# Value pass of a two-layer decoder trunk: a pair of chunks every five chunks, with the sums of rows made by accumulating transfers

## The chip, the core and the metric

The kernel runs on one core of one Trainium2 chip. A core has five engines with a queue of instructions each, which wait for each other only through semaphores: PE (TensorE, matrix products), DVE (VectorE), ACT (ScalarE), POOL (GpSimd) and SP (SyncE, which here only issues transfers). Sixteen DMA engines move data between HBM and the on-chip memory. The metric is device time of one execution in microseconds, lower is better.

## The reference, cut to what matters

Two layers; each is a token mixer with cross-attention, and then a channel mixer (`peer_ffn`) that picks 16 of 16384 experts per token and head and adds up their value rows:

```python
u = u_tab[eid]
act = gelu(einsum('nhkd,nd->nhk', u, xb))
coef = gw * act
return einsum('nhk,nhkd->nd', coef, v_tab[eid])
...
x = layer_norm(DN_ALPHA * x + y, ln2_g[i], ln2_b[i])
```

There are 256 tokens of 1024 channels, and everything is float32. The kernel does not gather rows. It computes a dense table of coefficients, 16384 experts by 256 tokens, zero where an expert was not chosen, and multiplies it with the whole table `v`. That product, 256 tokens x 16384 experts x 1024 channels, is the value pass.

## The kernel before, in words

`peer_layer` streams the table `u` in 128 chunks, then the table `v` in 128 chunks of 128 experts x 1024 channels (512 KB each). All float32 products are made in three passes: each operand is split into a rounded high part (ACT casts it, line 110 for a chunk, line 246 for coefficients) and the remainder (DVE subtracts, line 125 and line 247), and `mm3` (lines 184 to 186) adds high x high, high x low and low x high.

The value pass is the loop over `i` in `range(P)` from line 1285. In step `i`:

- `next` pumps the stream. It splits chunk `i + 2` into a buffer pair `wH`, `wL` (three of them, `HL_BUFS`), and issues on SP's queue as many loads as the five `raw` buffers allow (`RAW_BUFS`, counted by `n_flight`).
- `coef(i + 2)` splits the coefficients of chunk `i + 2`: 256 columns, 128 for each half of the tokens. They lie in `lo` (chunks 0 to 63) and `hi` (64 to 127), which are also free scratch space once a chunk has been used.
- `paired(i)` does the additional work for pairs, below.
- PE multiplies chunk `i`: two halves of tokens (`tt`) x two halves of channels x three passes = 12 matmuls with 512 columns, all accumulated in four banks of PSUM.

The order on each engine is the order in which this code issues; nothing is reordered. ACT and DVE can be two chunks ahead of PE, since a split waits only for the buffer that PE has finished with.

Pairs. Two neighbouring chunks `p` and `p + 1` form a two-by-two block product (two halves of tokens, two chunks, two halves of channels), which normally takes eight block products. For a pair the kernel takes seven, by the scheme of Strassen and Winograd: it needs four sums of coefficients `s` (128 columns each) and four sums of rows `t` (512 columns each), all split into high and low parts: `sh`, `sl`, `th`, `tl`, which live in `xHL`. Four of the products use sums; their results go to banks of their own (`m1`, `m5`, `m7`, `m6`), which DVE and ACT add into the result once after the last pair (`onto`, counted from `done`). With a0, a1 for the two halves of channels of chunk `p`, and b0, b1 for those of chunk `p + 1`, the row sums are t1 = a1 - a0, t3 = b1 - a1, t2 = t3 + a0 and t4 = b0 - t2. `owed` says in which step PE makes the four products of sums.

Before, a pair sits at chunks 8k + 2 and 8k + 3: 12 values of k in layer 0 (`PAIRS[0]`, without 10) and 13 in layer 1. DVE makes the four row sums in two steps from the two raw chunks (lines 1197, 1198, 1200 and 1201), which keep their `raw` buffers until then.

In layer 0 the stream also carries four parts of the memory tokens (`memT`, split by ACT and POOL, line 123) and four pieces of `wkv` (split by ACT and DVE), after the chunks listed in `MEM1`: 80, 82, 84, 86 and 113, 116, 119, 122. At step `CLOSE - 2` the pool that holds `lo` is closed, and its space goes to the buffers for these.

Of the kernel before, what the change touches and what calls it, by code (L numbers as in the profile page):

```python
# [8 lines left out]
F32R = mybir.dt.float32r  # L9
# [4 lines left out]
ALU = mybir.AluOpType  # L14
# [36 lines left out]
class Trunk:  # L51
# [32 lines left out]
    def pump(self, upto):  # L84
        nc = self.nc
        upto = min(upto, len(self.items))
        while self.n_split < upto:
            i = self.n_split
            self.load(i + 1)
            ap, n, dest, keep, cuts = self.items[i]  # L90
            r = self.loaded.pop(i)
            self.n_split += 1
            if keep is not None:
                self.kept[keep] = r
                continue
            if type(dest) is int:
                h, l = self.extra[dest]
            elif dest is None:
                h = self.hl.tile([P, D], F32R, name="wH")[:, :n]
                l = self.hl.tile([P, D], F32R, name="wL")[:, :n]  # L100
            else:
                h, l = dest()
            z = self.twin.get(i)
            if z is not None:
                if z == 0:
                    self.pair = [r, self.loaded[min(q for q in self.twin if q > i)]]
                n = min(n, 512 * (z + 1))
                cuts = [slice(0, n)]
            for c in cuts:
                (nc.vector.tensor_copy if self.cast_dve else nc.scalar.copy)(h[:, c], r[:, c])  # L110
            k = n if getattr(dest, "pool", False) else min(n, self.pool_cols)
            if len(cuts) > 1:
                for c in cuts:
                    e = (nc.vector, nc.gpsimd)[c.start > 0]
                    e.tensor_sub(l[:, c], r[:, c], h[:, c].bitcast(F32))
                k = n
            elif k and self.chained:
                nc.vector.tensor_sub(l[:, k:], r[:, k:], h[:, k:].bitcast(F32))  # L118
                k += 2
                nc.gpsimd.tensor_sub(l[:, :k], r[:, :k], h[:, :k].bitcast(F32))  # L120
                k = n
            elif k:
                nc.gpsimd.tensor_sub(l[:, :k], r[:, :k], h[:, :k].bitcast(F32))  # L123
            if k < n:
                rest = lambda l=l, r=r, h=h, c=slice(k, n): nc.vector.tensor_sub(l[:, c], r[:, c], h[:, c].bitcast(F32))  # L125
# [912 lines left out]
    def peer_layer(self, layer):  # L1038
        nc, tc, A = self.nc, self.tc, self.A
        with ExitStack() as ctx:  # L1040
# [118 lines left out]
            first = {8 * k + 2: k for k in PAIRS[layer]}  # L1159
            done = 8 * PAIRS[layer][-1] + 8  # L1160
            gl = cp.tile([P, T], F32, name="gl", bufs=1)
            th, tl = self.xHL[:, 0:3, :], self.xHL[:, 3:6, :]
            sh, sl = (self.xHL[:, f, :].rearrange("p (f t) -> p f t", f=4) for f in (6, 7))
            plain = lambda a: a.bitcast(F32)

            def sums32(k):
                old = hi if k > 8 else lo
                flat = lambda b: old[:, b:b + 2, :].rearrange("p a b -> p (a b)")
                return [flat(b) for b in (0, 2, 4, 6)], flat(8).rearrange("p (f t) -> p f t", f=4)

            def split_sums(k, f, n, s):
                old = hi if k > 8 else lo
                t = old[:, 2 * f:2 * (f + n), :].rearrange("p (f a) b -> p f (a b)", f=n)
                nc.vector.tensor_sub(tl[:, s:s + n], t, plain(th[:, s:s + n]))

            def cast_sums(k, f, n, s):
                old = hi if k > 8 else lo
                t = old[:, 2 * f:2 * (f + n), :].rearrange("p (f a) b -> p f (a b)", f=n)
                nc.scalar.copy(th[:, s:s + n], t)

            def paired(i):
                k, j = divmod(i, 8)
                if j == 0 and k - 1 in PAIRS[layer]:
                    cast_sums(k - 1, 3, 1, 0)
                if j == 7 and k + 1 in PAIRS[layer]:
# [5 lines left out]
                    nc.vector.tensor_add(s[:, 0], ua, ub)  # L1191
                if k in PAIRS[layer]:
                    t, s = sums32(k)
                    if j < 2:
                        (a0, a1), (b0, b1) = [[r[:, :512], r[:, 512:]] for r in self.pair]
                    if j == 0:
                        nc.vector.tensor_sub(t[0], a1, a0)
                        nc.vector.tensor_sub(t[1], b1, a1)
                    elif j == 1:
                        nc.vector.tensor_add(t[2], t[1], a0)  # L1200
                        nc.vector.tensor_sub(t[3], b0, t[2])
                        self.n_flight -= 2
                        self.load(len(self.items))
                    elif j == 4:
                        nc.scalar.copy(sh[:, 0:3], s[:, 0:3])
                        nc.scalar.copy(sh[:, 3], part(i - 1)[1])
                        nc.vector.tensor_sub(sl[:, 0:3], s[:, 0:3], plain(sh[:, 0:3]))
                        nc.vector.tensor_sub(sl[:, 3], part(i - 1)[1], plain(sh[:, 3]))
                        cast_sums(k, 0, 2, 0)
                    elif j == 5:  # L1210
                        split_sums(k, 0, 2, 0)
                        cast_sums(k, 2, 1, 2)
                    elif j == 6:
                        split_sums(k, 2, 1, 2)
                if j == 0 and k - 1 in PAIRS[layer]:
                    split_sums(k - 1, 3, 1, 0)
                q = hi[:, 0:2, :].rearrange("p a b -> p (a b)")

                def onto(t, h, src, scale=ALPHA):
# [21 lines left out]


            owed = {}
            for k, n in zip(PAIRS[layer], PAIRS[layer][1:] + [None]):
                e = 8 * k + 7
# [6 lines left out]
            def coef(i):  # L1252
                src = block(i)
                if i in first:
                    cH, cL = cp.tile([P, T], F32R, name="cH"), cp.tile([P, T], F32R, name="cL")
                    self.split_to(cH[:, :P], cL[:, :P], src[:, :P])
                    return cH, cL
                if i - 1 in first:
                    cH, cL = cp.tile([P, T], F32R, name="cH"), cp.tile([P, T], F32R, name="cL")
                    _, s = sums32(i // 8)  # L1260
                    nc.scalar.copy(cH[:, :P], src[:, :P])
                    nc.scalar.copy(cH[:, P:], s[:, 3])
                    nc.vector.tensor_sub(cL[:, :P], src[:, :P], plain(cH[:, :P]))
                    nc.vector.tensor_sub(cL[:, P:], s[:, 3], plain(cH[:, P:]))
# [20 lines left out]
            for i in range(P):  # L1285
# [22 lines left out]
                if i in first or i - 1 in first:  # L1308
                    (_, (h, l), (cH, cL)), = late
                    if i in first:  # L1310
                        mixed(m1, h[:, :512], l[:, :512], (cH[:, :P], cL[:, :P]), first[i])
# [7 lines left out]
                for k, m in owed.get(i, ()):  # L1319
                    if m == 3:  # L1320
                        mixed(y[1][0], th[:, 0], tl[:, 0], (sh[:, 3], sl[:, 3]))
                    else:
                        mixed((m5, m7, m6)[m], th[:, m], tl[:, m], (sh[:, m], sl[:, m]), k)
                late = []
            self.pool_cols = MIX_COLS
            if layer:
# [22 lines left out]
    def plan(self):  # L1349
# [24 lines left out]
        def tail(layer):  # L1374
# [7 lines left out]
                self.add(A["u"][layer, i], D)  # L1382
            for i in range(P):
                e = i - P + HL_BUFS + EXTRA
                if i % 8 in (2, 3) and i // 8 in PAIRS[layer]:
                    self.twin[len(self.items)] = i % 8 - 2
# [113 lines left out]
```

## Time and profile before

| | |
|---|---|
| median of 3 runs | 1813.54 us (1813.49 to 1814.55) |
| the profiled execution | 1813.66 us, span 1811.9 us |
| granted TensorE clock | 0.999 |
| PE busy | 1791.1 us, 99% of the span |
| DVE, ACT, POOL busy | 80%, 55%, 24% |
| read from HBM | 330.98 MB |
| SP-issued queue | 56.9% of 16 DMA engines over the span |

The span runs from the first to the last instruction; the execution's own time has some launch and end around it. Busy shares are averages over stages with different limits: in the search stages DVE and POOL have more to do, in the value pass less. The value pass of layer 0 runs from about 577 to 922 us, that of layer 1 from about 1461 to 1804 us. A row of a group of instructions gives line, engine, operation, output and inputs, shapes, count, then busy time in us, mean ns of one, and the idle time of its engine just before it with what ended that.

### The profile page before, as it was taken

The numbers are of one execution on the slowest core, as the hardware profiler recorded it, in microseconds if no ns is written. First come the engines' busy times: TensorE is split into PE (matmuls) and PEld (weight loads), VectorE is DVE, ScalarE is ACT, GpSimd is POOL, SyncE is SP. The second block draws the span as 40 slices with busy tenths as digits, with TensorE's granted clock in tenths as the row PEclk, the third lists the DMA queues.
The fourth block names the chain that finished last, engine by engine and source line by source line (L and its number), as shares of the span: only waits on it lengthen the run. The fifth ranks groups of instructions, "written<-read, shape, count | busy, mean of one in ns | idle before, by whom it ended". The sixth has DMA issues, their size and how long they took to land.

```text
span 1811.9 us, 33750 instructions
## 1 busy us (share of the span) xinstructions
PE 1791.1 (99%) x12735; PEld 1652.1 (91%) x12735; DVE 1451.5 (80%) x3035; ACT 993.4 (55%) x1766; POOL 430.9 (24%) x324
## 2 busy tenths in 40 slices
PE   8999999999999999999999999999999999999998
PEld 8999999999999888888898899999999988888886
DVE  6674769599998888878868748685999978888877
ACT  6554555455545666566657355555554456665653
POOL 2015772333332000010001368325333300000000
PEclk9999999999999999999999999999999999999999
DMA  7656565655555655565756355666555556555564
GB/s 241 208 160 193 172 194 191 197 167 163 162 164 164 208 198 198 197 210 190 243 177 186 114 179 177 197 191 186 161 163 164 164 175 212 198 199 192 186 209 128
DMA packets 95555, 334.22 MB, mean 184 GB/s; under 512 B 10652, under 2 KB 13728, under 8 KB 95136
## 3 DMA queue, kind: packets, MB, share of 16 engines
q1 hardware_dynamic: 93752, 328.93, 56.9%
q10 hardware_dynamic: 1640, 3.15, 0.5%
q8 instruction: 99, 1.62, 0.4%
q14 instruction: 64, 0.52, 0.1%
HBM read 330.98 MB, written 1.05 MB: 183 GB/s over the span
## 4 chain that ended last, share of the span: by engine, by line
PE 71%; issue 17%; POOL 7%; DVE 3%; ACT 1%; DMA 0%; POOLq 0%; SPq 0%; DVEq 0%; ACTq 0%
PE bank L186 23%; PE bank L185 23%; PE bank L184 23%; POOL wL L120 7%; PE bank L250 2%; ACT wH L110 1%; DVE eL L125 0%; DVE wL L125 0%; PE bank L344 0%; DVE eH L110 0%; POOL wL L123 0%; PE bank L243 0%; DMA raw<-in_w0kg_dram 0%; DMA cp<-in_rg_par_dram 0%; DVE x L297 0%
## 5 line engine op out<-in xcount | busy, mean ns | idle before, releaser
L110 ACT CAST wH<-raw 128x1024 fp32r<-128x1024 f32 (+3 forms) x605 | 615.9, 1019 | 689.6 <-PE bank L186 222.1
L184 PE MATMUL bank<-xHL,wH 128*128 128x256 f32 x2536 | 715.6, 282 | 5.0 <-ACT wH L110 5.0
L186 PE MATMUL bank<-xHL,wL 128*128 128x256 f32 x2536 | 702.2, 277 | 0.6 <-DVE wL L125 0.6
L185 PE MATMUL bank<-xHL,wH 128*128 128x256 f32 x2536 | 702.4, 277 | 0.0
L125 DVE TENSOR_TENSOR wL<-raw,wH 128x1024 fp32r<-128x1024 f32 (+3 forms) x413 | 451.7, 1096 | 276.1 <-ACT wH L110 274.4
L184 PEld LDWEIGHTS bank<-xHL,wH 128*128 128x128 f32 x2536 | 477.3, 188 | 5.0 <-ACT wH L110 5.0
L186 PEld LDWEIGHTS bank<-xHL,wL 128*128 128x128 f32 x2536 | 477.1, 188 | 1.1 <-DVE wL L125 0.8
L185 PEld LDWEIGHTS bank<-xHL,wH 128*128 128x128 f32 x2536 | 477.9, 188 | 0.0
L185 PE MATMUL bank<-wL,cH 128*128 128x512 f32 x890 | 346.4, 389 | 1.0 <-DVE wL L125 1.0
L186 PE MATMUL bank<-wH,cL 128*128 128x512 f32 x890 | 346.7, 390 | 0.0
L184 PE MATMUL bank<-wH,cH 128*128 128x512 f32 x890 | 345.9, 389 | 0.0
L123 POOL TENSOR_TENSOR wL<-raw,wH 128x1024 fp32r<-128x1024 f32 (+1 forms) x121 | 256.0, 2120 | 209.3 <-ACT wH L110 208.8
L185 PEld LDWEIGHTS bank<-wL,cH 128*128 128x128 f32 x890 | 167.0, 188 | 37.7 <-DVE wL L125 2.5
L186 PEld LDWEIGHTS bank<-wH,cL 128*128 128x128 f32 x890 | 167.0, 188 | 35.3
L184 PEld LDWEIGHTS bank<-wH,cH 128*128 128x128 f32 x890 | 167.1, 188 | 35.0
L120 POOL TENSOR_TENSOR wL<-raw,wH 128x386 fp32r<-128x386 f32 x126 | 129.8, 1030 | 279.8 <-DVE wL L118 279.8
L333 POOL TENSOR_TENSOR x<-x,raw 128x256 f32<-128x256 f32 x6 | 4.9, 819 | 545.9 <-ACT x L330 545.9
L1000 DVE TENSOR_TENSOR oh<-iota,i12T 128x1024 f16<-128x1024 f16 x128 | 130.5, 1019 | 0.0
L118 DVE TENSOR_TENSOR wL<-raw,wH 128x640 fp32r<-128x640 f32 x126 | 104.0, 825 | 7.4
L1003 DVE TENSOR_TENSOR oh<-oh,gT 128x1024 f16<-128x1024 f16 x128 | 90.0, 703 | 4.4
L1133 PE MATMUL bank<-oh 128*128 128x128 f16 x1024 | 81.1, 220 | 1.1 <-DVE oh L1003 1.1
L1133 PEld LDWEIGHTS <-oh 128*128 128x128 f16 x1024 | 58.9, 98 | 6.0 <-DVE oh L1003 1.5
(340 smaller groups left out, 1989.8 us busy)
## 6 DMA issues: line engine op xcount, KB each, us to landing
raw<-in_u_dram SPq DMA_DIRECT2D x256, 512.0 KB, 3.6
raw<-in_v_dram SPq DMA_DIRECT2D x256, 512.0 KB, 4.1
raw<-in_w_q_dram SPq DMA_DIRECT2D x32, 512.0 KB, 4.2
raw<-in_w_out_dram SPq DMA_DIRECT2D x16, 512.0 KB, 4.0
raw<-in_w0qx_dram SPq DMA_DIRECT2D x8, 512.0 KB, 5.0
raw<-in_wkv_dram SPq DMA_DIRECT2D x8, 512.0 KB, 5.7
raw<-in_w0v_dram SPq DMA_DIRECT2D x8, 384.0 KB, 5.7
raw<-in_w0o_dram SPq DMA_DIRECT2D x8, 384.0 KB, 3.0
```

Source lines behind the costliest of these rows:

```text
L110: (nc.vector.tensor_copy if self.cast_dve else nc.scalar.copy)(h[:, c], r[:, c])
L118: nc.vector.tensor_sub(l[:, k:], r[:, k:], h[:, k:].bitcast(F32))
L120: nc.gpsimd.tensor_sub(l[:, :k], r[:, :k], h[:, :k].bitcast(F32))
L123: nc.gpsimd.tensor_sub(l[:, :k], r[:, :k], h[:, :k].bitcast(F32))
L125: rest = lambda l=l, r=r, h=h, c=slice(k, n): nc.vector.tensor_sub(l[:, c], r[:, c], h[:, c].bitcast(F32))
L184: mm(out, sH, mH, start=start, stop=False, skip_group_check=True)
L185: mm(out, sH, mL, start=False, stop=False, skip_group_check=True)
L186: mm(out, sL, mH, start=False, stop=stop, skip_group_check=True)
L250: self.nc.tensor.matmul(out, lhsT, rhs, start=start, stop=stop, skip_group_check=True)
L1000: nc.vector.tensor_tensor(flat(oh[:, 1:3]), self.iota2.unsqueeze(1).to_broadcast([P, 4, P, 2]), pairs(self.i12T[:, j]), op=ALU.is_equal)
L1003: nc.vector.tensor_tensor(flat(oh[:, 0:2]), two.rearrange("p z (q e t) -> p z q e t", q=2, t=2), pairs(self.gT[:, j]), op=ALU.mult)
L1133: nc.tensor.matmul(wp[:, qs], oh[:, 2, q // 2, :, q % 2], oh[:, z, q // 2, :, q % 2], start=z == 0, stop=z == 1, skip_group_check=True)
```

## The change

Pairs now start at chunk 8 and then at every fifth chunk from 16: up to 96 in layer 0 (18 pairs) and up to 106 in layer 1 (20 pairs).

The row sums are no longer made by DVE. At step p - 2 SP loads a0 a second time, straight into t2; ACT writes the negated chunk, -a0 and -a1, into t1 and t3; and POOL issues two transfers that add a1 from HBM to t1 and b1 to t3 in place. At step p - 1 ACT writes -b0 into t4, and POOL issues two transfers within the on-chip memory: t3 is added to t2, then t2 is added to t4. So t4 comes out with its sign turned; the coefficient that it meets (`s[:, 3]`) is negated by ACT to fit. The transfers are issued in that order from POOL's queue, and each waits for what it reads.

ACT and DVE then split the sums: t1, t3 at step p + 2 and p + 3, t2 at p + 3 and p + 4, t4 at p + 5, into the place of t1 in `th` and `tl`. The products of sums are owed at p + 4, at the next pair's first step (two), and one step later; for the last pair at p + 4 and p + 5.

The row sums of neighbouring pairs use two regions of `lo` or `hi` in turn, the coefficient sums one. The coefficients of chunk p + 1 are overwritten in place with tb - s2, so that `coef` splits them like any others. A raw chunk of a pair is given back in the step in which it is negated. `MEM1` moves to 109, 111, ... 123, and `CLOSE` to 84.

```diff
-PAIRS = [[1, 2, 3, 4, 5, 6, 7, 8, 9, 11, 12, 13], list(range(1, 14))]
-CLOSE = 76
-MEM1 = (80, 82, 84, 86, 113, 116, 119, 122)
+PAIRS = [[8] + list(range(16, 97, 5)), [8] + list(range(16, 107, 5))]
+CLOSE = 84
+MEM1 = (109, 111, 113, 115, 117, 119, 121, 123)
...
-                if z == 0:
-                    self.pair = [r, self.loaded[min(q for q in self.twin if q > i)]]
+                self.pair[z] = r
...
+            def old(p, b, n):
+                t, b = (lo, b) if p + 5 < CLOSE - 2 else (hi, b)
+                return t[:, b:b + n, :].rearrange("p a b -> p (a b)")
+
+            def sums_c(p):
+                return old(p, 0, 2)
+
+            def sums_r(p):
+                b = 8 * (first[p] % 2) + 2
+                return [old(p, b, 4), old(p, b + 4, 2), old(p, b + 6, 2)]
...
+                if i - 2 in first:
+                    c, (t13, _, _) = sums_c(i - 2), sums_r(i - 2)
+                    nc.scalar.copy(sh, c)
+                    nc.scalar.copy(th[:, 0:2], t13.rearrange("p (f a) -> p f a", f=2))
+                    nc.vector.tensor_sub(sl, c, plain(sh))
+                if i - 3 in first:
+                    t13, t2, _ = sums_r(i - 3)
+                    nc.scalar.copy(th[:, 2], t2)
+                    nc.vector.tensor_sub(tl[:, 0:2], t13.rearrange("p (f a) -> p f a", f=2), plain(th[:, 0:2]))
+                if i - 4 in first:
+                    _, t2, _ = sums_r(i - 4)
+                    nc.vector.tensor_sub(tl[:, 2], t2, plain(th[:, 2]))
+                if i - 5 in first:
+                    _, _, t4 = sums_r(i - 5)
+                    nc.scalar.copy(th[:, 0], t4)
+                    nc.vector.tensor_sub(tl[:, 0], t4, plain(th[:, 0]))
+                if i + 3 in first:
                     (ta, ua), (tb, ub) = part(i + 3), part(i + 4)
-                    _, s = sums32(k + 1)
+                    s = four(sums_c(i + 3))
+                    nc.scalar.mul(s[:, 3], ub, -1.0)
                     nc.vector.tensor_sub(s[:, 1], ta, ua)
                     nc.vector.tensor_sub(s[:, 2], ub, s[:, 1])
-                    nc.vector.tensor_sub(s[:, 3], tb, s[:, 2])
                     nc.vector.tensor_add(s[:, 0], ua, ub)
-                    if j == 0:
-                        nc.vector.tensor_sub(t[0], a1, a0)
-                        nc.vector.tensor_sub(t[1], b1, a1)
-                    elif j == 1:
-                        nc.vector.tensor_add(t[2], t[1], a0)
-                        nc.vector.tensor_sub(t[3], b0, t[2])
...
+                    nc.vector.tensor_sub(ub, tb, s[:, 2])
+
+                if i + 2 in first:
+                    p = i + 2
+                    t13, t2, _ = sums_r(p)
+                    t1, t3 = t13[:, :512], t13[:, 512:]
+                    nc.sync.dma_start(t2, V[layer, p][:, :512])
+                    nc.scalar.mul(t13, self.pair[0], -1.0)
+                    nc.gpsimd.dma_start(t1, V[layer, p][:, 512:], accum_op=ALU.add)
+                    nc.gpsimd.dma_start(t3, V[layer, p + 1][:, 512:], accum_op=ALU.add)
+                    self.n_flight -= 1
+                    self.load(len(self.items))
+                if i + 1 in first:
+                    t13, t2, t4 = sums_r(i + 1)
+                    nc.scalar.mul(t4, self.pair[1][:, :512], -1.0)
+                    nc.gpsimd.dma_start(t2, t13[:, 512:], accum_op=ALU.add)
+                    nc.gpsimd.dma_start(t4, t2, accum_op=ALU.add)
+                    self.n_flight -= 1
+                    self.load(len(self.items))
...
-                for m, at in enumerate((e, 8 * n + 2, 8 * n + 2, 8 * n + 3) if n else (e, e, e, e + 1)):
-                    owed.setdefault(at, []).append((k, m))
+                for m, at in enumerate((p + 4, n, n, n + 1) if n else (p + 4, p + 5, p + 5, p + 5)):
+                    owed.setdefault(at, []).append((p, m))
```

More of the change, by code (lines that the diff above doesn't have):

```diff
@@ L1158, in peer_layer @@
             part = lambda i: [block(i)[:, :P], block(i)[:, P:]]
-            first = {8 * k + 2: k for k in PAIRS[layer]}
-            done = 8 * PAIRS[layer][-1] + 8
+            first = {p: n for n, p in enumerate(PAIRS[layer])}
+            done = PAIRS[layer][-1] + 6
             gl = cp.tile([P, T], F32, name="gl", bufs=1)
             th, tl = self.xHL[:, 0:3, :], self.xHL[:, 3:6, :]
-            sh, sl = (self.xHL[:, f, :].rearrange("p (f t) -> p f t", f=4) for f in (6, 7))
+            sh, sl = self.xHL[:, 6, :], self.xHL[:, 7, :]
@@ L1176, in cast_sums @@
[L1176 to L1179, printed above, removed]
-            def paired(i):
[L1182 to L1185, printed above, removed]
+            four = lambda a: a.rearrange("p (f t) -> p f t", f=4)
@@ L1310, in peer_layer @@
                     if i in first:
-                        mixed(m1, h[:, :512], l[:, :512], (cH[:, :P], cL[:, :P]), first[i])
+                        mixed(m1, h[:, :512], l[:, :512], (cH[:, :P], cL[:, :P]), i)
                     else:
@@ L1318, in peer_layer @@
                             products(tt, 512 * k, 512, late)
-                for k, m in owed.get(i, ()):
+                for p, m in owed.get(i, ()):
+                    stat = four(sh)[:, m], four(sl)[:, m]
                     if m == 3:
-                        mixed(y[1][0], th[:, 0], tl[:, 0], (sh[:, 3], sl[:, 3]))
+                        mixed(y[1][0], th[:, 0], tl[:, 0], stat)
                     else:
-                        mixed((m5, m7, m6)[m], th[:, m], tl[:, m], (sh[:, m], sl[:, m]), k)
+                        mixed((m5, m7, m6)[m], th[:, m], tl[:, m], stat, p)
                 late = []
@@ L1384, in tail @@
                 e = i - P + HL_BUFS + EXTRA
-                if i % 8 in (2, 3) and i // 8 in PAIRS[layer]:
-                    self.twin[len(self.items)] = i % 8 - 2
+                if i in PAIRS[layer] or i - 1 in PAIRS[layer]:
+                    self.twin[len(self.items)] = int(i not in PAIRS[layer])
                 self.add(A["v"][layer, i], D, e if layer and 0 <= e < EXTRA else None)
```

39 lines of the change are left out of this document (2 added, 37 removed).

## The prediction

> **What bounds the kernel now.** I read the page first: busy shares, then the chain that ended last.
>
> ```profile
> span 1811.9 us, 33750 instructions
> PE 1791.1 (99%) x12735; PEld 1652.1 (91%) x12735; DVE 1451.5 (80%) x3035; ACT 993.4 (55%) x1766; POOL 430.9 (24%) x324
> PE 71%; issue 17%; POOL 7%; DVE 3%; ACT 1%; DMA 0%; POOLq 0%; SPq 0%; DVEq 0%; ACTq 0%
> ```
>
> PE is busy 99% of the span. That alone does not say it is the limit in the stage that changes, so next comes the view of busy time by stage, with the steady part of the value pass of each layer. Its columns are length, then busy us of PE, PEld, DVE, ACT and POOL, granted clock, DMA share, GB/s.
>
> ```profile
> 600.00:900.00 300.00, 299.71 (x1317) 246.82 (x1316) 253.62 (x402) 183.99 (x306) 8.81 (x6) 1.00 0.62 206
> 1480.00:1780.00 300.00, 299.72 (x1317) 246.71 (x1316) 252.49 (x413) 181.43 (x306) 0.00 (x0) 1.00 0.60 198
> ```
>
> PE is without a gap in both, at clock 1.00. DVE has 15% left, ACT 39%, POOL nearly everything, the DMA engines 38%. So a matmul taken out of this stage is worth its pitch, as long as none of the others runs out. The pitch is read from starts in the timeline of PE, since durations overlap:
>
> ```profile
> 699.65 0.39 PE L186 MATMUL bank<-wH,cL 128*128 128x512 f32 x1
> ...
> 701.01 0.39 PE L186 MATMUL bank<-wH,cL 128*128 128x512 f32 x1
> ```
>
> Six matmuls from 699.65 to 701.01, that is 0.227 us each. A normal chunk is 12 of them, 2.72 us. The same timeline shows the pass's stalls, one at the first pair of each layer:
>
> ```profile
> 606.33 0.39 PE L184 MATMUL bank<-wH,cH 128*128 128x512 f32 x1
> 607.00 0.50 PE L185 MATMUL bank<-wL,cH 128*128 128x512 f32 x1 [0.28 <-DVE wL L125]
> 607.34 0.49 PE L186 MATMUL bank<-wH,cL 128*128 128x512 f32 x1
> 607.67 0.40 PE L184 MATMUL bank<-wH,cH 128*128 128x512 f32 x1
> ```
> ```profile
> 1490.07 0.39 PE L184 MATMUL bank<-wH,cH 128*128 128x512 f32 x1
> 1490.74 0.50 PE L185 MATMUL bank<-wL,cH 128*128 128x512 f32 x1 [0.28 <-DVE wL L125]
> ...
> 1491.41 0.40 PE L184 MATMUL bank<-wH,cH 128*128 128x512 f32 x1
> ```
>
> Three pitches should take 0.68 us; they take 1.34 both times, so 0.66 us is lost, while DVE makes the row sums of the first pair before it splits the chunk that PE needs.
>
> **PE's part.** A pair takes 21 matmuls in place of 24. Pairs go from 12 to 18 in layer 0 and from 13 to 20 in layer 1: 13 more, 39 matmuls less, 39 x 0.227 = 8.85 us. A five-chunk period is then 5 x 12 - 3 = 57 matmuls, 12.9 us; everything else must fit into that.
>
> **DVE and ACT.** Mean durations, from the groups of instructions in 600 to 900 us, shapes kept apart:
>
> ```profile
> L125 DVE TENSOR_TENSOR wL<-raw,wH 128x1024 fp32r<-128x1024 f32 x101 | 123.5, 1223 | 40.5 <-ACT wH L110 39.9
> L110 ACT CAST wH<-raw 128x1024 fp32r<-128x1024 f32 x101 | 106.3, 1052 | 86.2 <-PE bank L186 70.5 <-issue 15.7
> L247 DVE TENSOR_TENSOR cL<-wglo,cH 128x256 fp32r<-128x256 f32 x40 | 16.7, 418 | 0.0
> L246 ACT CAST cH<-wglo 128x256 fp32r<-128x256 f32 x40 | 16.0, 401 | 0.0
> L1179 ACT CAST xHL<-wglo 128x512 fp32r<-128x512 f32 x16 | 9.9, 619 | 0.0
> L1174 DVE TENSOR_TENSOR xHL<-wglo,xHL 128x1024 fp32r<-128x1024 f32 x8 | 9.7, 1218 | 0.0
> L1179 ACT CAST xHL<-wglo 128x1024 fp32r<-128x1024 f32 x8 | 8.4, 1047 | 0.0
> L125 DVE TENSOR_TENSOR wL<-raw,wH 128x512 fp32r<-128x512 f32 x12 | 8.2, 684 | 0.0
> L1197 DVE TENSOR_TENSOR wglo<-raw 128x512 f32<-128x512 f32 x8 | 5.5, 684 | 0.0
> L246 ACT CAST cH<-wglo 128x128 fp32r<-128x128 f32 x6 | 1.8, 297 | 0.0
> L1207 DVE TENSOR_TENSOR xHL<-wglo,xHL 128x384 fp32r<-128x384 f32 x8 | 4.4, 552 | 0.0
> L1205 ACT CAST xHL<-wglo 128x384 fp32r<-128x384 f32 x8 | 4.1, 508 | 0.0
> L1191 DVE TENSOR_TENSOR wglo<-wglo 128x128 f32<-128x128 f32 x7 | 2.0, 283 | 0.0
> ```
>
> DVE before, per eight chunks: splits 7 x 1.22 + 0.68, coefficients 6 x 0.42 + 3 x 0.28, four coefficient sums 4 x 0.28, four row sums 4 x 0.68, their splits 1.22 + 2 x 0.68, and those of the coefficient sums 0.55 + 0.28: 19.9 of 21.1 us, 94%. After, per five: 4 x 1.22 + 0.68, 4 x 0.42 + 0.28, 4 x 0.28, no row sums, 1.22 + 2 x 0.68, and 0.68 for the coefficients: 11.9 of 12.9, 92%. These sums overstate (starts are closer than durations), but equally. More pairs and fewer sums cancel: DVE is no tighter, and its burst of four 0.68 us sums within two steps is gone.
>
> ACT before: 7 x 1.05 + 0.62, 6 x 0.40 + 3 x 0.30, then 0.51 + 0.30 for the coefficient sums and 1.05 + 2 x 0.62 for the row sums: 14.4 of 21.1, 68%. After: 4 x 1.05 + 0.62, 4 x 0.40 + 0.30, 0.62, 1.05 + 2 x 0.62, plus three negations (1024, 512 and 128 columns, taken like the casts: 1.05, 0.62, 0.30): 11.6 of 12.9, 90%. ACT loses most of its air. It is hidden by the buffers: ACT and DVE work two chunks ahead of PE, and in the groups ACT's idle time before the 1024 cast is ended mostly by PE freeing a buffer (70.5 of 86.2 us). The new wait for t4 and the reuse of `th[0]` stand behind the cast of the same step, which waits for nearly the same matmuls.
>
> **The transfers.** Here nothing in the trace is alike: POOL issues no DMA, nothing accumulates. Per pair come one SP load of half a row (256 KB, t2) and four POOL transfers of 256 KB. The nearest rows are in the DMA view, 600 to 900 us in 40 slices of 7.5 us:
>
> ```profile
> DMA  3955737628628628548456375488396286386588
> GB/s 102 337 183 172 258 133 247 230 84 318 181 72 341 195 85 308 185 134 287 142 204 226 129 243 190 156 300 291 97 338 187 88 298 199 127 293 209 155 228 269
> q1 hardware_dynamic: 17149, 61.40, 61.3%
> raw<-in_v_dram SPq DMA_DIRECT2D x112, 512.0 KB, 4.1
> raw<-in_memT_dram SPq DMA_DIRECT2D x4, 256.0 KB, 3.2
> ```
>
> Bandwidth: five chunks are 2.62 MB, five halves 1.31 MB, in 12.9 us 304 GB/s. Slices reached 337 to 341 GB/s, and 206 at 61% extrapolates to 336. So 304 fits. If an accumulating transfer costs its bytes twice, the demand is 385 GB/s: over 341, though the slice at 341 is itself marked only 8 tenths, which leaves room to about 400. The Trainium skill, "DMA: Bandwidth & Descriptors", Rules for kernel authors, says that an accumulate reads its destination and writes it later; by that the second figure is the one to use, and no run here shows it yet.
>
> Latency: there is a loop. ACT negates a row into t1 and t3 (step p-2), POOL adds to both (D13), then adds t3 to t2 (D2), ACT copies t2 into `th[2]` (0.62 us) at p+3, and the next negation (1.05 us) stands right behind that copy on ACT. So D13 + D2 + 1.7 must not exceed 12.9: D13 + D2 up to 11.2 us is free. Beyond, each us is paid in each of the 34 five-chunk intervals (16 in layer 0, 18 in layer 1), because casts queue behind that copy. Lower end: at the 256 KB price, 3.2 + 0.9 for the second transfer + 3.2 = 7.3. Upper end: three transfers one after the other at the 512 KB price, 12.3. I take the 512 KB price for each hop, as the destination's bytes count too, with t1 and t3 overlapped: 4.1 + 2 x 0.9 + 4.1 = 10.0, inside the limit by 1.2. The third hop, t4, is needed by PE only some 19 us after the negation (two more steps, and 6 matmuls), against 10.0 + 4.1 + 0.62 + 0.68 = 15.4.
>
> The Trainium skill, same page, Latency and other measured facts, puts the first byte of a POOL-issued transfer at about 1 us against 0.6 for SP; three issues would add an estimated 1.2 us to the 10.0, which is just the margin.
>
> **What is moved.** SP gets one issue per pair ahead of the next loads; they run five buffers deep, 12.9 us ahead of a 4.1 us landing, so it costs nothing. POOL's queue holds its four transfers and, in layer 0, the splits of memory tokens: moved from chunks 80 to 86 to 109 to 115, behind the last accumulation at step 95, so neither blocks the other. Chunks 109 to 123 carry no row sums: with a wkv item ACT needs 1.05 + 0.40 + 1.05 of 2.72, DVE 2.86 in one step but 4.5 in two, of 5.4. Without that cover, four DVE splits, 4.9 us. Closing the left half at 84 rather than 76 matters to nobody before 109.
>
> **The sum.** Profiled execution 1813.66 (span 1811.9 and 1.8 around it), 0.12 above the median. Less 8.85; less half of the two first-pair stalls, 0.65, since the burst is gone, but the pair now starts two chunks sooner: 1804.2, as a median 1804.0.
>
> **Rivals.**
> 1. *The loop does not fit.* With D13 + D2 at the upper end 12.3, 1.1 us x 34 = 37 us is lost: 1813.5 - 9.5 + 37 = 1841. It decides from 11.2 us. For it: two of the hops read SBUF in queues shared with loads that already land in 4.1. Against: 1.2 us of margin.
> 2. *The DMA engines run out.* 385 GB/s against 341: the period is 14.6 us, 1.7 x 34 = 57, 1861. For it the double bytes, against it the 8-tenths slice.
> 3. *POOL issues late beside DVE.* The row of POOL's own work in this kernel:
>
> ```profile
> L123 POOL TENSOR_TENSOR memL<-raw,memH x8: 1307/1664/2497, 29.8 to 800.8; 128x512 fp32r<-128x512 f32 x8
> ```
>
> One shape takes 1.31 to 2.50 us, so POOL can be held for 1.2 us. Three issues held so make 13.6 of the 10.0: 2.4 x 34 = 82, 1886. Against it: an issue need not read as this subtraction does. The Trainium skill, "SBUF — State Buffer", Who interferes with whom, states that descriptors made on GpSimd starve while DVE runs a two-port instruction, but that a tensor_tensor does not block descriptor writing; by that page this rival falls.
> 4. *ACT at 90% is too tight.* A stall of 0.25 us per pair, 38 pairs, eats 9.5: 1813. For it the 90% and in-order coupling; against it the overstated sum.
>
> **How the numbers follow.** Forecast 0.52, with its own range 1802.5 to 1808. Rival 4 takes 0.12 (0.04 still faster, 0.06 same, 0.02 slower), rival 1 0.17, rival 2 0.12, rival 3 0.07. Faster by over 0.2% (3.6 us, about what can be told from no change): 0.56; same 0.06; slower 0.38. Forecast, rival 4 and rival 1 are 0.81, so the range goes from 1802.5 (both stalls gone entirely, and a little) to 1845.
>
> **What would show it.** PE: 39 matmuls less, no wait in the value pass beyond a few tenths of a us. DMA view: POOL's queue with transfers of 256 KB landing in about 4 us, share under 1. ACT's `th[2]` copy waiting for DMA, if at all, for less than a us. Wrong, if that copy or the 1024 negation carries waits of us for a transfer, PE shows a gap in every period, and the five-chunk distance grows beyond 12.9 us.

## The result, and the profile after

The changed kernel takes 1964.76 us (median; 1964.1 to 1967.71) beside 1813.59 us for the kernel before: a ratio of 1.0835, interval 1.0817 to 1.0854. It is 151 us slower, and 161 us above the forecast of 1804.0. The part of the page with spans, busy times and DMA queues:

```profile
span 1962.4 us, 34419 instructions
PE 1847.2 (94%) x12696; PEld 1678.2 (86%) x12696; DVE 1431.8 (73%) x2989; ACT 1073.0 (55%) x1882; POOL 562.4 (29%) x476
q1 hardware_dynamic: 99224, 338.89, 52.5%
q0 software_dynamic: 21888, 39.86, 12.5%
```

PE has 39 matmuls less, as forecast, but it is no longer full. Queue q0, which did not exist before, holds the accumulating transfers of the row sums: 39.86 MB, a tenth of all bytes, but 12.5 of the 65 per cent of DMA time.

The steady part of both value passes, in the view of busy time by stage (columns as in the prediction: length, PE, PEld, DVE, ACT, POOL, clock, DMA share, GB/s):

```profile
650.00:950.00 300.00, 260.34 (x1036) 205.88 (x1035) 194.36 (x306) 176.77 (x289) 59.74 (x66) 0.93 0.81 222
1600.00:1900.00 300.00, 252.84 (x982) 198.86 (x981) 186.56 (x306) 175.69 (x290) 59.37 (x68) 0.90 0.83 226
```

No engine is full here on average: PE went from 300 to 260 and 253 us, DVE is at two thirds, the DMA engines at 0.8. Where nothing is full on average and time is lost in every period, a circle of waits is the first thing to look for. From their first to their last matmul the two value passes took 341.7 and 343.4 us before; now they take 410.4 and 423.2. That is 148.6 of the 151 us.

The circle can be read from one period, in the timelines of ACT and of POOL (start, duration, engine, line, what it does, and in brackets the idle time ahead and what ended it; ... marks rows left out). L1212 is the negation into t1 and t3, L1213 and L1214 the additions to them, L1220 and L1221 those to t2 and t4, L1185 the copy of t1 and t3 into `th`, L1189 the copy of t2:

```profile
704.39 1.05 ACT L1212 ACTIVATE wglo<-raw 128x1024 f32<-128x1024 f32 x1
...
717.37 1.05 ACT L1185 CAST xHL<-wglo 128x1024 fp32r<-128x1024 f32 x1 [3.05 <-DMA wglo<-in_v_dram]
...
722.10 0.62 ACT L1189 CAST xHL<-wglo 128x512 fp32r<-128x512 f32 x1 [2.77 <-DMA wglo<-wglo]
722.63 1.06 ACT L1212 ACTIVATE wglo<-raw 128x1024 f32<-128x1024 f32 x1
```
```profile
705.74 0.87 POOL L1213 DMA_DIRECT2D wglo<-in_v_dram  x1 [0.49 <-ACT wglo L1212]
706.28 1.22 POOL L1214 DMA_DIRECT2D wglo<-in_v_dram  x1
717.55 0.86 POOL L1220 DMA_DIRECT2D wglo<-wglo  x1 [10.05 <-DMA wglo<-in_v_dram]
722.62 0.86 POOL L1221 DMA_DIRECT2D wglo<-wglo  x1 [4.20 <-issue]
```

The negation ends at 705.44. POOL issues t1 and t3 at once, but t3 has landed only at 717.3: 11.8 us, the longest of all 38. Then t2 is issued, lands at 722.08, is copied, and the next negation starts at 722.63, 18.24 us after the last one. The forecast had 12.9 here. Over all 34 five-chunk intervals the distance between negations is 17.5 us on average (16.1 to 19.3); from a negation's end to t3's landing it is 9.4 (7.8 to 11.8), and for t2, from issue to landing, 6.1. 9.4 + 6.1 + 1.7 is 17.2, and the rest are starts of a few tenths. The loss beyond the forecast is (17.46 - 12.94) x 34 = 154 us.

The average DMA share hides where in the period the transfers stand. Here is the first hop, from the end of the negation to t3's landing, and then the last 3 us up to the end of the next negation (columns as above):

```profile
705.44:717.30 11.86, 8.67 (x28) 6.99 (x29) 8.65 (x14) 6.67 (x12) 1.76 (x2) 0.71 0.97 259
720.68:723.68 3.00, 3.00 (x15) 2.47 (x14) 0.53 (x1) 1.58 (x3) 0.86 (x1) 1.00 0.02 4
```

From the issue of t1 to the landing of t3 the packets take at least 0.95 of the time of the 16 DMA engines in each of the 38 pairs: t1, t3 and the previous pair's t4 share them with loads of chunks, 1.5 MB on average. When these have landed, little is left to move until the next negation gives a buffer back: in the last 3 us up to its end the share is 0.13 on average of the 34 intervals. So the engines are full in the hop that the circle waits for, and nearly idle at the end of the period.

Who waits is shown by the view of waits over the whole run (who waited, for what; us in total, times, longest):

```profile
POOL wglo L1220 <- DMA wglo<-in_v_dram: 186.5, 24, 10.1
ACT xHL L1189 <- DMA wglo<-wglo: 113.1, 28, 5.8
PE bank L184 <- DVE xHL L1193: 89.9, 35, 3.6
```

POOL's wait is the first hop (7.8 us each time), ACT's the second; PE's, for the split behind ACT's copy, is what is paid, in 35 of 38 pairs. How PE pays stands in its timeline:

```profile
708.63 0.79 PE L184 MATMUL bank<-xHL 128*128 128x512 f32 x1 [3.59 <-DVE xHL L1193]
709.22 0.63 PE L185 MATMUL bank<-xHL 128*128 128x512 f32 x1
709.65 0.63 PE L183 MATMUL bank<-wH,cH 128*128 128x512 f32 x1
710.08 0.63 PE L184 MATMUL bank<-wL,cH 128*128 128x512 f32 x1
...
713.06 0.63 PE L185 MATMUL bank<-xHL 128*128 128x512 f32 x1
713.49 0.53 PE L183 MATMUL bank<-wH,cH 128*128 128x512 f32 x1
713.85 0.39 PE L184 MATMUL bank<-wL,cH 128*128 128x512 f32 x1
```

After a gap of 3.59 us the matmuls start 0.43 us apart instead of 0.227, from 709.22 to 713.49, ten pitches; the rows of the stages show the same as a granted clock of 0.93 and 0.90. Added up over all starts of PE in the two passes, 112 us beyond the normal pitch are gaps and 41 us matmuls at half the clock. The half clock is a consequence of the gaps: it does not add to the 154, since the circle, not PE, sets the period. The Trainium skill, "TensorE: Matmul & The Clock Gate", What's actually happening, states that the clock falls to half after an idle window of about 3.4 us and comes back after one as long that is busy; the gap of 3.59 us and the 4.3 us at half pitch agree roughly with it.

### The profile page after: what moved, and what is told of

It is laid out like the page before. It is cut to its first block, busy times and chain, and to the rows that moved or that the text cites. A ratio compares the mean times of both kernels' runs of the same rounds, so it can differ in the third digit from the quotient of the medians.

```text
span 1962.4 us, 34419 instructions
## 1 busy us (share of the span) xinstructions
PE 1847.2 (94%) x12696; PEld 1678.2 (86%) x12696; DVE 1431.8 (73%) x2989; ACT 1073.0 (55%) x1882; POOL 562.4 (29%) x476
## 3 DMA queue, kind: packets, MB, share of 16 engines
q0 software_dynamic: 21888, 39.86, 12.5%
## 5 line engine op out<-in xcount | busy, mean ns | idle before, releaser
L109 ACT CAST wH<-raw 128x1024 fp32r<-128x1024 f32 (+2 forms) x605 | 607.3, 1005 | 538.7 <-POOL wL L119 186.4
L124 DVE TENSOR_TENSOR wL<-raw,wH 128x1024 fp32r<-128x1024 f32 (+3 forms) x413 | 445.8, 1081 | 420.0 <-ACT wH L109 418.7
L184 PE MATMUL bank<-wL,cH 128*128 128x512 f32 (+1 forms) x825 | 333.1, 404 | 1.3 <-DVE wL L124 1.3
L185 PE MATMUL bank<-wH,cL 128*128 128x512 f32 (+1 forms) x825 | 332.7, 403 | 0.0
L183 PE MATMUL bank<-wH,cH 128*128 128x512 f32 (+1 forms) x825 | 332.7, 403 | 0.0
L184 PEld LDWEIGHTS bank<-wL,cH 128*128 128x128 f32 x825 | 161.8, 196 | 38.5 <-DVE wL L124 2.9
L185 PEld LDWEIGHTS bank<-wH,cL 128*128 128x128 f32 x825 | 161.9, 196 | 36.0
L184 PE MATMUL bank<-xHL 128*128 128x512 f32 x152 | 72.1, 474 | 91.0 <-DVE xHL L1193 89.9
L184 PEld LDWEIGHTS bank<-xHL 128*128 128x128 f32 x152 | 32.8, 216 | 113.2 <-DVE xHL L1193 103.8
L1220 POOL DMA_DIRECT2D wglo<-wglo x28 | 24.2, 864 | 213.2 <-DMA wglo<-in_v_dram 186.5
```

What stands on the lines that cost most here:

```text
L183: mm(out, sH, mH, start=start, stop=False, skip_group_check=True)
L184: mm(out, sH, mL, start=False, stop=False, skip_group_check=True)
L185: mm(out, sL, mH, start=False, stop=stop, skip_group_check=True)
L1220: nc.gpsimd.dma_start(t2, t13[:, 512:], accum_op=ALU.add)
```

## The experiments

Theory A: an accumulating transfer occupies the DMA engines twice as long as a plain one of the same bytes, and so the first two hops, beside the loads, no longer fit into 12.9 us. Rivals: the order of issue (negation and t4 behind t2 in their queues), the mere number of transfers, or a compute engine. The times of e1_plain, e3_cut and e7_thin2 are of one execution each.

**e1_plain: the same transfers, without the addition.**

```diff
-nc.gpsimd.dma_start(..., accum_op=ALU.add)
+nc.gpsimd.dma_start(...)                      # all four
```

> The four POOL transfers of each pair become plain copies: same rows, same queue, same waits, but nothing is added, so the row sums are wrong. Theory A (an accumulating transfer moves its bytes twice, and this is what makes the loop from the negation over t3 and t2 to the next negation too long): a 2 KB row takes about 84 to 93 ns of a DMA engine in place of 200, the loop falls from a mean of 17.6 us to 13 us or less, the time to 1804 to 1820. Theory B (POOL-issued transfers are slow in themselves, whatever they do): the loop stays above 16 us, the time above 1910.

It took 1807.66 us, beside 1813.68 for the kernel before. Queue q0 on its page and its steady stage:

```profile
q0 software_dynamic: 12160, 39.86, 5.9%
```
```profile
650.00:900.00 250.00, 250.00 (x1098) 205.74 (x1097) 205.53 (x316) 185.63 (x299) 38.84 (x63) 1.00 0.84 284
```

PE is full again; the first hop takes 6.1 us, the second 4.9, and negations stand 13.1 us apart (means). The landings of t1 and t3 in the view of DMA issues (size, median us to landing), first in the changed kernel from 650 to 950 us, then here from 650 to 900:

```profile
wglo<-in_v_dram POOLq DMA_DIRECT2D x22, 256.0 KB, 7.9
```
```profile
wglo<-in_v_dram POOLq DMA_DIRECT2D x20, 256.0 KB, 5.0
```

The bytes are the same 39.86 MB, the time on the 16 DMA engines 5.9% of 1805.9 = 107 us against 12.5% of 1962.4 = 245: the addition makes a byte cost 2.3 times as much. The packets are cut differently, too: with the addition each row of 2 KB is a packet, which takes 178 ns of an engine (median), without it two rows make one of 4 KB, which takes 159. The size of the packets is not the reason, since the plain rows of 2 KB on SP's queue in the changed kernel take 84 ns. Number of transfers, order, ACT and POOL are the same in both kernels, so the addition is the cause. The run also gives what the pair count is worth when nothing else is in the way: 6.0 us, not 9.5.

**e2_eight: the change with pairs every eight chunks.** If the circle alone is the loss, it vanishes when it has 21 us.

```diff
-PAIRS = [[8] + list(range(16, 97, 5)), [8] + list(range(16, 107, 5))]
+PAIRS = [list(range(8, 97, 8)), list(range(8, 105, 8))]
```

> Accumulating transfers as in the change, but a pair every eight chunks, 12 and 13 pairs, so no matmul less than before. If the cost is a loop that must close before the next pair (17.6 us against eight chunks of 21.1 us), it is hidden: 1811 to 1815, with the 0.66 us stall of the first pair gone. If each pair's transfers cost something by themselves (the 160 us lost over 38 pairs are 4.2 us each), 25 pairs cost 105 us: about 1918.

It took 1831.03 us, ratio 1.0091 (1.0074 to 1.0108): between the two expectations. Its waits, 600 to 950 us:

```profile
ACT xHL L1189 <- DMA wglo<-wglo: 29.1, 9, 5.4
ACT xHL L1185 <- DMA wglo<-in_v_dram: 20.1, 8, 3.7
```

The next negation is far away now (eight chunks, 93 matmuls, are 21.1 us), and yet the copies of t1, t3 and t2 still wait, and about 0.8 us a pair reaches PE, 19.6 us over the two passes. A second limit had been overlooked: inside a pair the copies stand at the steps p+2 and p+3, four and five steps behind the negation, whatever the distance of the pairs. In e1_plain, where ACT hardly waits, they start 7.1 to 9.1 and 10.2 to 13.2 us after the negation's end; here, between 690 and 890 us, the sums arrive 9.0 to 11.0 and 14.0 to 16.1 us after it. The limit inside the pair is as tight as the circle.

**e3_cut: the order of issue.** The negation stands ahead of t2's copy, and t4's addition behind the next t1 and t3, so that the circle is cut.

```diff
 if i - 3 in first:
-    nc.scalar.copy(th[:, 2], t2)                      # moved below the block "i + 2 in first"
 ...
+if i - 3 in first:
+    nc.scalar.copy(th[:, 2], t2)
+    nc.gpsimd.dma_start(t4, t2, accum_op=ALU.add)
 if i + 1 in first:
-    nc.gpsimd.dma_start(t4, t2, accum_op=ALU.add)
```

> The loop is opened, everything else as in the change: ACT negates the next pair's chunk before it copies t2, and POOL issues the addition of t2 to t4 behind the next pair's t1 and t3, so only t1 and t3 must land before the next negation. If latency alone holds the pair: loop = landing of t3 after the negation (9 to 11 us) + 3.3 us of ACT, so 12.9 to 14 us, 1804 to 1845. If the DMA engines' time is the limit, the period stays at what their packets take (32 x 200 + 40 x 182 + 8 x 93 ns = 14.4 us) or above, with their share near 100%: 1855 or more.

It took 1993.34 us, more than the change itself. In ACT's timeline the copy of t4 (L1195 in this kernel) now carries the wait:

```profile
747.91 0.62 ACT L1195 CAST xHL<-wglo 128x512 fp32r<-128x512 f32 x1 [5.04 <-DMA wglo<-wglo]
766.47 0.62 ACT L1195 CAST xHL<-wglo 128x512 fp32r<-128x512 f32 x1 [5.51 <-DMA wglo<-wglo]
```

They stand 18.6 us apart. t4's addition, issued at 757.32 among the next t1 and t3, took until 766.37 to land: 9 us (8.4 is the median of all 38), where t4's lands in 3.6 (median) in the changed kernel, which issues it ahead of the next t1 and t3. The order of issue alone is no way out: the wait moved to the next deadline. The forecast for a limit by latency was missed by far; the time is in the range given for full DMA engines (1855 or more), but their share in the steady stage is 0.81 and not near 1.

**e4_half: half of the additions.** DVE makes t1 and t3, DMA adds to t2 and t4 only.

```diff
-nc.scalar.mul(t13, self.pair[0], -1.0)
-nc.gpsimd.dma_start(t1, V[layer, p][:, 512:], accum_op=ALU.add)
-nc.gpsimd.dma_start(t3, V[layer, p + 1][:, 512:], accum_op=ALU.add)
+nc.vector.tensor_sub(t1, a[:, 512:], a[:, :512])                                  # step p-2
+nc.vector.tensor_sub(t13[:, 512:], self.pair[1][:, 512:], self.pair[0][:, 512:])  # step p-1
...
```

> DVE makes t1 and t3 from the raw chunks as before the change; t2 and t4 stay accumulating transfers, pairs every five chunks. The loop has one hop left (t2, about 6 us) and the DMA engines 11.2 us of 12.9. If loop and DMA engines were the cause, 1803 to 1810. If DVE (10.7 us by starts, plus 2 x 0.6) is now too tight for PE, a stall of 0.3 to 1 us per pair: 1815 to 1840.

It took 1809.84 us, ratio 0.9977 (0.9967 to 0.9987); taken again as e11_half2 on another chip, 1809.79, ratio 0.998 (0.997 to 0.9989). With the longest hop gone the five-chunk period holds:

```profile
650.00:900.00 250.00, 250.00 (x1097) 205.49 (x1096) 222.49 (x344) 173.88 (x285) 33.28 (x35) 1.00 0.83 257
```

> e4_half once more, more rounds, beside the two others on the same chip: 1808 to 1811, faster than before by 0.1 to 0.3%.

The DMA share is 0.83, as in the changed kernel, while PE has no gap. So a high share is not the bound by itself; a hop on which ACT waits is.

**e5_late: eight chunks, and later deadlines.** e2_eight, with every use of the sums two steps later.

```diff
-if i - 2 in first: ... i - 3 ... i - 4 ... i - 5
+if i - 4 in first: ... i - 5 ... i - 6 ... i - 7
-for m, at in enumerate((p + 4, n, n, n + 1) if n else (p + 4, p + 5, p + 5, p + 5)):
+for m, at in enumerate((p + 6, n, n, n + 1) if n else (p + 6, p + 7, p + 7, p + 7)):
...
```

> As e2_eight (a pair every eight chunks, all sums by accumulating transfers), but each sum is split, and its product made, two steps later. If the 17 us of e2_eight come from the distance inside a pair (t1 and t3 used four steps after the negation, t2 five), two more steps of 2.7 us cover landings that were 3 to 4 us late: 1811 to 1814. If the busy DMA engines (85%) delay something else, such as the loads of chunks, it stays at 1825 to 1831.

It took 1815.1 us, ratio 1.0006 (0.9996 to 1.0015): of the 17 us of e2_eight about one is left, which the interval does not tell from none.

```profile
650.00:900.00 250.00, 250.00 (x1100) 206.38 (x1099) 187.69 (x273) 165.42 (x261) 41.01 (x43) 1.00 0.88 252
```

PE is full at a DMA share of 0.88, the highest of all these kernels, with all four additions still there. t3 still lands 9.4 us after the negation, as in the change; only nothing waits for it now. That settles e2_eight: its loss was distance inside the pair, not bandwidth. It also shows that accumulating sums buy nothing at eight chunks, since DVE was not the bound there.

**e6_dve: five chunks, all four sums on DVE.**

```diff
+nc.vector.tensor_sub(t1, a1, a0); nc.vector.tensor_sub(t3, b1, a1)                # step p-2
+nc.vector.tensor_add(t2, t13[:, 512:], a0); nc.vector.tensor_sub(t4, t2, b0)      # step p-1
...
```

> Pairs every five chunks as in the change, but all four row sums made by DVE as before it, so no transfers beside the loads of chunks. If DVE's time by starts (10.7 us + 4 x 0.6 = 13.1 of 12.9 us) decides, every pair costs PE 0.2 to 0.5 us: 1815 to 1825, slower than before. If the two chunks of lead hide that, 1806 to 1809.

It took 1819.39 us, ratio 1.0029 (1.0018 to 1.004), inside the range expected if DVE decides. DVE has 233 of 250 us:

```profile
650.00:900.00 250.00, 248.52 (x1074) 200.30 (x1073) 233.12 (x368) 161.19 (x266) 8.32 (x6) 1.00 0.60 204
```

The five-chunk period therefore does need some of the sums off DVE; 15.8 us of stalls in the two passes are more than the 39 matmuls save.

**e7_thin2: the change with thinner loads.** Chunks 8 to 111 are loaded by half, the other half read twice.

```diff
-for c in cuts:                                                       # the load of a chunk
+for c in [slice(0, 512)] if self.n_load in self.thin else cuts:
...
```

> The change with the loads of chunks 8 to 111 cut to their first half (256 KB in place of 512 KB); casts, splits and negations read that half twice, so every engine has the same work, but the values are wrong. If t1 and t3 land late because their packets share the DMA engines with the loads, their landing falls from 8.5 us to 6 to 7 and the loop below 14 us: 1808 to 1840. If an accumulating transfer has this latency by itself, the loop stays above 16 us: above 1910.

It took 1854.68 us, between the two expectations. Negations are 14.5 us apart (five-chunk intervals), the hops take 7.7 and 4.8 us:

```profile
650.00:900.00 250.00, 234.44 (x995) 188.47 (x994) 186.42 (x296) 168.99 (x278) 57.16 (x63) 0.98 0.73 174
```

So of the change's 151 us about 110 go with half of the load traffic, and 41 stay. The additions and the loads beside them lengthen the hop together: taking the additions out, or half of the loads, brings most of the time back. The loads arrive in bursts, too. They wait on SP's queue for the negation that reads their buffer, and then go out together beside t1 and t3 (waits of SP's queue in the changed kernel, over the whole run, 5 us each time):

```profile
SPq L138 <- ACT wglo L1212: 120.2, 24, 6.8
```

**e8_pool: t2 and t4 computed by POOL.** No transfers beside the loads of chunks.

```diff
+nc.vector.tensor_sub(t1, ...); nc.vector.tensor_sub(t13[:, 512:], b1, a1)
+nc.gpsimd.tensor_add(t2, t13[:, 512:], a0); nc.gpsimd.tensor_sub(t4, t2, b0)
...
```

> Pairs every five chunks; DVE makes t1 and t3, POOL makes t2 and t4 with two subtractions or additions of 512 columns, no accumulating transfers. If POOL and DVE do not hold each other, POOL's 2 x 1.7 us are hidden and this gives 1806 to 1809. If each POOL instruction holds DVE for its 1.3 us or more, DVE needs 11.9 + 2.6 of 12.9 us: 1.6 us per pair, 1850 to 1870.

It took 1870.85 us, ratio 1.0311 (1.0294 to 1.0328), at the upper edge of what was expected if POOL and DVE hold each other. Groups of instructions, 650 to 900 us, shapes apart:

```profile
L1217 POOL TENSOR_TENSOR wglo<-wglo,raw 128x512 f32<-128x512 f32 x11 | 24.2, 2199 | 118.9 <-DVE wglo L1216 118.9
L1218 POOL TENSOR_TENSOR wglo<-wglo,raw 128x512 f32<-128x512 f32 x11 | 14.8, 1343 | 0.9
L246 DVE TENSOR_TENSOR cL<-wglo,cH 128x256 fp32r<-128x256 f32 x30 | 21.3, 712 | 0.0
L1197 DVE TENSOR_TENSOR xHL<-wglo,xHL 128x512 fp32r<-128x512 f32 x12 | 21.2, 1766 | 0.0
```

Both engines hold each other: the same shape takes POOL 1.34 us in one line and 2.20 in the other, and DVE 0.71 instead of 0.42 us (256 columns) and 1.77 instead of 0.68 (512). The mean of 0.71 is a mixture: those of the 256-column form that overlap one of POOL's take 1.5 us (median), the others 0.42. The Trainium skill, "SBUF — State Buffer", Who interferes with whom, states that a two-input DVE operation contends with GpSimd's reads; these rows agree.

**e9_three: one addition left.** DVE makes t1, t3 and t2, and only t4 accumulates, whose deadline is the latest.

```diff
 nc.vector.tensor_sub(t13[:, 512:], b1, a1)
+nc.vector.tensor_add(t2, t13[:, 512:], a0)
+nc.scalar.mul(t4, b0, -1.0)
 nc.gpsimd.dma_start(t4, t2, accum_op=ALU.add)
...
```

> Pairs every five chunks, DVE makes t1, t3 and t2, only t4 stays an accumulating transfer (one per pair, no second load of a half chunk). DVE by starts: 10.7 + 3 x 0.6 = 12.5 of 13.0 us. If DVE's limit lies between four sums (which cost 12 us against the copies of e1_plain) and two, this one decides: 1808 to 1810 if three still fit, 1811 to 1816 if in-order waits already cost PE 0.1 to 0.2 us per pair.

It took 1807.45 us (1806.9 to 1808.06), ratio 0.9965 (0.9952 to 0.9978): faster by 0.35% than the kernel before, a little below the expectation, and 2.3 us below e11_half2 on the same chip.

```profile
650.00:900.00 250.00, 250.00 (x1098) 205.66 (x1097) 229.94 (x358) 172.14 (x285) 20.34 (x20) 1.00 0.70 226
```

DVE is at 92% and PE still full; one sum less on DVE is what separates it from e6_dve. It reaches e1_plain's 1807.66, so nothing of what the pair count gives is lost any more.

**e10_six: e4_half with pairs every six chunks.** It was to show whether more room makes e4_half quicker still.

```diff
-PAIRS = [[8] + list(range(16, 97, 5)), [8] + list(range(16, 107, 5))]
+PAIRS = [[8] + list(range(16, 97, 6)), [8] + list(range(16, 107, 6))]
```

> e4_half with a pair every six chunks: 32 pairs in place of 38, 18 matmuls more than e4_half (4.1 us), DMA engines at about 75% in place of 83%. If e4_half is at the worth of its matmuls, this is 3 to 4 us slower than e4_half and about equal to the kernel before: 1810.5 to 1813. If the busy DMA engines cost e4_half something, less of that shows: 1808 to 1810.

It took 1837.98 us, ratio 1.0133 (1.0117 to 1.0148): a miss by 25 us. Its stage and its largest wait of ACT, 600 to 950 us (L1196 is the copy of t4):

```profile
650.00:900.00 250.00, 244.44 (x1039) 194.73 (x1038) 197.53 (x303) 153.84 (x256) 29.54 (x30) 0.99 0.73 229
```
```profile
ACT xHL L1196 <- DMA wglo<-wglo: 39.5, 12, 3.9
```

In e4_half the same copy waits 5.9 us in 7 times. t2's addition lands in the same time in both kernels (7.8 us), t4's in 6.1 instead of 4.8. The issue of t2 at p-1 and the copy of t4 at p+5 are fixed steps of a pair, and with six chunks only 69 matmuls lie between them where with five there are 72, since step p-1 is then no longer the one that also carries the first of the last pair's recombined products: 0.7 us less room, and 1.3 us more latency. The DMA share of 0.73 in the stage says little of this hop: while t4's addition is under way the share is 0.87 (0.85 in e4_half), and 1.5 MB of chunk loads pass beside it instead of 1.0 (means). That fits its later landing, but no run takes these loads away, so the reason stays open.

## Why the prediction was wrong

**PE: confirmed in number, smaller in worth.** The 39 matmuls went, but e1_plain, in which nothing else stands in the way, gains 6.0 us and not 9.5. Of the missing 3.5, about 1.5 are a pitch of 228.1 ns instead of 227.6 over the 2958 matmuls of the two passes: it is there in e6_dve, which has no extra transfers, and not in e5_late, which has all of them but 25 pairs, so it goes with the number of pairs. In e1_plain the next start stands about 231 ns behind a matmul of the sums and 227.5 behind the others; why is not shown. The rest are stalls, of which 0.65 was to go: in e1_plain all stalls of the two passes are 0.94 and 2.87 us, where before they were 0.66 and 2.11.

**DVE: confirmed.** It was to be at 92% by durations that overstate; in e1_plain it is at 82%, and beyond the first pair no wait of PE for a DVE that was merely busy appears in e1_plain's stage. **ACT at 90% (rival 4): refuted** by e1_plain too, which has all of ACT's new work and PE at 250.00 of 250.00.

**Bandwidth (rival 2): the double bytes right, the consequence wrong.** The prediction left open whether an accumulating transfer costs its bytes twice. It does, 2.3 times by e1_plain, and so the larger demand of 385 GB/s was the one to use. The Trainium skill, "DMA: Bandwidth & Descriptors", Rules for kernel authors, says that the destination is read and written later; the measured price points the same way. But over a period the DMA engines did not run out: the share is 0.81 and 0.83, and e5_late is without a gap at 0.88. They are full inside the first hop, and there they lengthen the loop. Nothing of the period of 14.6 us that this rival gave is seen; the period is longer, because the engines stand nearly idle at its end.

**The loop: the step that failed.** The mechanism was named (rival 1) with its place, its limit of 11.2 us, its 34 payments and its sign in the trace: the copy of t2 waiting for DMA for us, a gap in every period. All of that came. What failed is the term "4.1 + 2 x 0.9 + 4.1 = 10.0", taken from landings of plain loads at a DMA share of 0.62. Measured were 9.4 + 6.1 = 15.5. Two things were left out of it, and the runs price them apart. Plain transfers under the load of this stage take 6.1 + 4.9 = 11.0 (e1_plain), which uses up nearly all of the 11.2 already; the addition makes 15.5 of that. With half the loads the same additions take 7.7 + 4.8 = 12.5 (e7_thin2). The upper end of 12.3, which set rival 1's 1841 and so the top of the range at 1845, was no upper end either: it had three plain landings in a row, but no longer landing in a stage that the change itself makes fuller. With the measured distance the forecast's own sum nearly comes out: 1804.0 + 34 x 4.52 + 3.5 = 1961.2, beside 1964.8; of the 3.6 us left, 1.2 lie in the two eight-chunk intervals (21.9 and 21.7 us instead of 21.2), the rest ahead of the first and behind the last negation of each pass. Rival 1 also had the hops share queues with the loads. They do not: POOL's transfers have q0, the loads q1, and it is the DMA engines that they share. With the first bytes of the Trainium skill, "DMA: Bandwidth & Descriptors", Latency and other measured facts, the prediction's estimate was 11.2; no run tells how much of the 11.0 of e1_plain is first bytes and how much load.

**The deadline inside the pair: overlooked.** The prediction tested the circle and t4's chain (15.4 of 19 us), but not that t1, t3 and t2 have only some 8.5 and 11 us from the negation to their copies at any spacing; e2_eight and e5_late showed it at 16 us, at a spacing where the circle does not bind. At five chunks both limits are one path, so the sum above holds. The t4 chain, held to be safe, decided in e3_cut and e10_six; in the changed kernel t4 lands 20.0 us after the negation, where the prediction had 14.1, but the longer period covers that.

**POOL held by DVE (rival 3): refuted.** The issues on POOL took 0.86 to 1.22 us in the rows above. POOL's long waits are for landings, not for DVE. Its subtraction is indeed held by DVE, as e8_pool shows, but an issue does not behave like one.

**What was costed at nothing.** POOL's queue is in order, and t2's addition, waiting up to 10 us for t3, holds whatever follows it there; no run prices that by itself. SP's issue of half a row shows no price either, but SP's loads wait for the negation (24 times, 5 us each), which makes them a burst beside t1 and t3. Memory tokens and the closing of the left half cost nothing that the traces show.

## What to carry to other kernels

Price a chain of transfers by its landings under the load that the new kernel will have, not under that of the old one, and an accumulating transfer at more than twice its bytes (2.3 times here); a loop with 1 us of margin on durations from a lighter stage had none. A DMA share averaged over a period says little of the moment in which a transfer is waited for: look at the share between issue and landing. Besides the distance to the next round, check every deadline inside a round, in steps from issue to use. Here the work that came off the full engine was best moved in the smallest part that freed it, the part with the latest deadline: one addition of four moved to DMA gave 6.3 us, two gave 4, all four cost 151, and none cost 5.

## What the runs showed that was not expected

- An accumulating row of 2 KB takes 178 ns of a DMA engine (median) beside 84 for a plain one on SP's queue, and the additions to t1 and t3 land in 7.4 to 8.1 us (medians by tile, changed kernel and e2_eight) beside 5.0 without the addition.
- More room made a kernel slower: six chunks instead of five cost 28 us (e10_six beside e4_half), with 0.7 us less between t2's issue and t4's copy, and t4 landing 1.3 us later for a reason that stays open.
- PE stayed without a gap at DMA shares of 0.83 to 0.88, and had 13 to 16% of gaps at 0.81 to 0.83. The share of a stage does not tell whether transfers bound it; who waits for them does. Inside the hop that was waited for, the share was at least 0.95.
